# All rows of attention scores in the two double PSUM buffers of a planned decoder layer, and four changed rules of its planner

## The chip, the core and the metric

The kernel runs on one core of a Trainium2 chip. The core has a matrix engine (TensorE; the profile has PE for its matmuls and PEld for its weight loads), a vector engine (VectorE, DVE), a scalar engine (ScalarE, ACT), GpSimd (POOL) and a queue that issues transfers (SyncE, SP). Matmuls write to PSUM, which VectorE and ScalarE read; everything else lies in SBUF. The metric is the time of one execution in microseconds on the device. Each execution is one program, and the profile shows one of them.

## The reference

One decoder layer on 1024 tokens of width 1024: a norm, one input projection, a recurrent branch (convolution, two gates, a scan), a latent attention branch of 8 heads, an output projection over both, a SwiGLU FFN of width 2816, and a gated per-layer embedding. What matters here is the attention:

```python
s = jnp.einsum('bqhd,bkhd->bhqk', qn, k_nope)          # 64 wide
s = s + jnp.einsum('bqhr,bkr->bhqk', qr, k_rope)       # 32 wide
s = jnp.where(k_idx <= q_idx, s * ATT_SCALE, -inf)     # causal
pr = softmax(s, axis=-1)
out = jnp.einsum('bhqk,bkhd->bqhd', pr, v)
```

## The kernel before

Everything is float32. A float32 operand is split into a rounded part and a rest (tiles `x_h` and `x_l`, or `q_h` and `q_l`), and a product is three matmuls: high by high, high by low, low by high. Tiles hold 128 rows of features by 1024 tokens.

The attention works by head (0 to 7) and by block of 128 queries (`qb` 0 to 7). The function `scores` takes one such block: the scores of 128 queries against the `n` = 128 (`qb` + 1) keys that the causal mask leaves, 128 to 1024 columns in PSUM (tile `s`). TensorE writes them in three matmuls of up to 512 columns, or six, with one more of 128 columns that adds the mask (`s<-mb,ib`). VectorE takes the negative maximum of each row (`nm<-s`), and ScalarE the exponential with the row's sum (`pA<-s,nm` for the blocks up to 512 columns, `pB<-s,nm` for the longer ones). Only then may the PSUM buffer of these scores be used again. The exponentials are transposed in blocks of 128 by TensorE (tile `tp`), copied and split by ScalarE and VectorE (tile `pt`), and multiplied with the values into tile `av`, which ScalarE and VectorE then move to `ya`. Beside this run, for the heads to come, the products that make queries (`qps`, then `qf`, `q_h`, `q_l`) and keys (`kps`, then `k_h`, `k_l`), at the start the values (`v`), and at the end the output projection of the recurrent half (`wo`), after its operands were split (`yr_h`, `yr_l`). After each second head its normalisation is spread over the partitions (`rbc`).

PSUM has eight banks of 512 columns. `NWIDE` = 2 (L369) makes four of them two double buffers of 1024 columns (pool `wide`); the other four are single (pool `bank`). Before, a block of scores of over 512 columns takes a double buffer, and one of up to 512 a single bank, from the pool that `tp`, `av`, `qps`, `kps`, `v` and `rbc` use too.

The order of the instructions is not that of the code. The kernel records every operation (`Plan.add`), and `Plan.order` (L239) lays them out by list scheduling, once, before the program is built: it keeps a clock for each engine, takes of the operations that are ready and have their buffers the one with the lowest key (its place in the code, with a few shifts), and lets it last as long as `Plan.cost` says (L167). The table `LAT` (L133) has how much later another engine sees an operation's end: 0.25 us from VectorE to TensorE and 0.11 from ScalarE to TensorE, for instance. A buffer comes free at `b.done`, after its last user (L329). Each engine then runs its own instructions strictly in the order that the plan gave, waiting on semaphores for the others. Since all instructions are emitted in one helper, all have the same line in the profile, L361, and are told apart by their tiles; in the changed kernel, three lines longer there, it is L364.

Of the kernel before, what the change touches and what calls it, by code (L numbers as in the profile page):

```python
# [19 lines left out]
HB = 512  # L20
# [120 lines left out]
class Plan:  # L141
# [25 lines left out]
    def cost(self, eng, fn, a, k, out):  # L167
        w = out.width() if isinstance(out, View) else 0
        if fn == "dma_start":
            v = k["out"] if isinstance(k["out"], View) else k["in_"]  # L170
            return v.shape[0] * v.width() * 4 / 360e3, 2.1
        if eng == "tensor":
            if fn == "transpose":
                return 0.108, 0.18
            return w * 0.000417 + 0.0135, 0.18
        if eng == "vector":
            if fn == "reciprocal":
                return 0.065 + w * 0.0063, 0.13
            if fn in ("tensor_reduce", "reduce_sum"):
                return 0.065 + k["in_"].width() * 0.00104, 0.13  # L180
            ptr = 0.061 * any(isinstance(x, View) for x in (k.get("scalar"), *a[2:])) if fn == "scalar_tensor_tensor" else 0.0
            one = fn in ("tensor_copy", "tensor_scalar", "tensor_scalar_mul", "tensor_scalar_add", "tensor_scalar_max")
            if one and all(v.buf.tag not in PS for v in [*a, *k.values()] if isinstance(v, View)):
                return 0.068 + w * 0.00052, 0.13
            return 0.068 + ptr + w * 0.00104, 0.13
        if eng == "scalar":
            src = k["in_"] if "in_" in k else a[1]
            c = (0.052 if src.buf.tag in PS else 0.093) + w * 0.000833
            c += 0.093 * sum(isinstance(k.get(n), View) for n in ("scale", "bias"))
            c += 0.2 * isinstance(k.get("accum_out"), View)  # L190
            return c, 0.14
        return 0.15 + w * (0.0033 if fn == "tensor_copy" else 0.0022), 0.14
# [10 lines left out]
    def add(self, eng, fn, a, k):  # L203
        o = Op()
        o.eng, o.fn, o.a, o.k, o.idx = eng, fn, a, k, len(self.ops)
        o.succ, o.npred, o.ready = [], 0, 0.0
        out = k["out"] if "out" in k else a[0]
        outs = [v for v in (out, k.get("accum_out")) if isinstance(v, View)]
        rest = list(a[1:] if "out" not in k else a) + [v for n, v in k.items() if n not in ("out", "accum_out")]
        ins = [v for v in rest if isinstance(v, View)]  # L210
        o.cost, o.lat = self.cost(eng, fn, a, k, out)
        o.port = self.shares(eng, fn, ins)
        f = k.get("func") or next((x for x in a if isinstance(x, AF)), None)
        o.table = f.name if eng == "scalar" and f is not None and f.name in FIRST else None
        preds = {self.hold: True} if self.hold else {}
        for v, w in [(v, False) for v in ins] + [(v, True) for v in outs]:
            p0, p1, c0, c1 = v.region
            keep = []
            for (q, r, qw) in v.buf.log:
                hit = r[0] < p1 and p0 < r[1] and r[2] < c1 and c0 < r[3]  # L220
                if hit and (w or qw) and q is not o:
                    preds[q] = True
                if not (w and q is not o and p0 <= r[0] and r[1] <= p1 and c0 <= r[2] and r[3] <= c1):
                    keep.append((q, r, qw))
            keep.append((o, v.region, w))
            v.buf.log = keep
        o.key = o.idx + self.shift + OFF.get(eng[0] + out.buf.name.rstrip('_ab') if isinstance(out, View) else '', 0) + (DEF if eng in ('vector', 'scalar') and not any(v.buf.tag == 'bank' for v in ins + outs) else 0)
        o.bufs = list(dict.fromkeys(v.buf for v in ins + outs))
        for b in o.bufs:
            if not b.left:  # L230
                b.first = o.idx
            b.left += 1
        for q in preds:
            q.succ.append(o)
            o.npred += 1
        self.ops.append(o)
        return o

    def order(self):  # L239
# [28 lines left out]
        while left:  # L268
            while frees and frees[0][0] <= t:
                _, _, tag, n = heapq.heappop(frees)  # L270
                free[tag] += n
            moved = False
            for e in names:
                while future[e] and future[e][0][0] <= t:
                    _, i, o = heapq.heappop(future[e])
                    heapq.heappush(avail[e], (o.key, i, o))
                if busy[e] > t or not avail[e]:
                    continue
                pick, skipped, best = None, [], None
                tries = 0  # L280
                while avail[e] and tries < 40:
                    i, _, o = heapq.heappop(avail[e])
                    tries += 1
                    ok = all(b.placed or free[b.tag] > min(unplaced(b), RES.get(b.tag, 99)) for b in o.bufs)
                    if ok:
                        key = i
                        if e == "scalar" and o.table and o.table not in SAME.get(table, ()):
                            key = i + SWITCH
                        if best is None or key < best[0]:
                            if best is not None:  # L290
                                skipped.append((best[1], best[2].idx, best[2]))
                            best = (key, i, o)
                        else:
                            skipped.append((i, o.idx, o))
                        if e != "scalar" or key == i:
                            break
                    else:
                        skipped.append((i, o.idx, o))
                for s in skipped:
                    heapq.heappush(avail[e], s)  # L300
                if best is None:
                    continue
                o = best[2]
                moved = True
                start = t
                c = o.cost
                if o.port:
                    start = max(t, port)
                    port = start + c
                if o.table and o.table not in SAME.get(table, ()):  # L310
                    table = FIRST[o.table]
                    c += 1.28
                for b in o.bufs:
                    if b.placed:
                        continue
                    b.placed = True
                    free[b.tag] -= 1
                    q, d = queue[b.tag], ahead[b.tag]
                    d[b.pos] = True
                    while head[b.tag] < len(q) and d[head[b.tag]]:  # L320
                        head[b.tag] += 1
                busy[e] = start + c
                o.end = start + c + o.lat
                o.st = start
                out.append((t, o.idx, o))
                left -= 1
                for b in o.bufs:
                    b.left -= 1
                    b.done = max(getattr(b, "done", 0.0), o.end)  # L329
                    if not b.left:  # L330
                        heapq.heappush(frees, (b.done, b.pos, b.tag, 1))
                for s in o.succ:
                    s.npred -= 1
                    r = start + c + (LAT[e, s.eng] if (e, s.eng) in LAT else o.lat)
                    s.ready = max(s.ready, r)
                    if not s.npred:
                        heapq.heappush(future[s.eng], (s.ready, s.idx, s))
            nxt = [busy[e] for e in names if busy[e] > t and (avail[e] or future[e])]
            nxt += [future[e][0][0] for e in names if future[e] and future[e][0][0] > t]
            if frees:  # L340
                nxt.append(frees[0][0])
            nxt = [x for x in nxt if x > t]
            if not left:
                break
            if not nxt:
                raise RuntimeError("the plan does not fit")
            t = min(nxt)
# [22 lines left out]
PS = ("bank", "wide")  # L370
# [6 lines left out]
def hybrid_layer(ctx, tc, xT, pT, pos, vec, const, const2, w1, wn, wrg, wq, wkv, wo, wg, wu, *rest):  # L377
# [252 lines left out]
    for k in range(8):  # L630
# [29 lines left out]
        for i in range(2):  # L660
            c = slice(i * P, (i + 1) * P)
# [215 lines left out]
    def scores(hd, qb):  # L877
# [7 lines left out]
        (qh, ql), (kh, kl) = qs[hd], ks[hd]  # L885
        n = (qb + 1) * P
        cc = slice(qb * P, (qb + 1) * P)
        ps = wide("s") if n > HB else bank("s")
        for c0 in range(0, n, HB):
            c1 = min(c0 + HB, n)  # L890
            T.matmul(ps[:, c0:c1], lhsT=qh[:, cc], rhs=kh[:, c0:c1], start=True, stop=False)
# [608 lines left out]
```

## Time and profile before

| | us |
|---|---|
| median of three timed runs | 1231.26 (1230.91 to 1231.33) |
| the profiled execution | 1228.91 |
| span of its instructions | 1227.1 |
| TensorE busy with matmuls | 1172.6 (96%) |
| VectorE busy | 990.7 (81%) |
| ScalarE busy | 648.5 (53%) |
| GpSimd busy | 249.8 (20%) |

The page's second part cuts the span into 40 slices of 30.7 us:

```profile
PE   8999999999999999999999999999599999999995
DVE  7878777777888699988888888867689758776998
ACT  8347857777855365454454444444232213476665
PEclk9999999999999999999999999999799999999998
```

Each digit is the busy share in tenths, and PEclk the clock that TensorE was granted. The attention is in slices 6 to 11, where VectorE and ScalarE stand at seven to eight tenths as well; the FFN fills slices 13 to 33. A busy share is not a bound by itself: matmuls are pipelined, and the record of one overlaps the next. Waits have to be read from the timeline of a stretch.

### The profile page before, as it was taken

Reading aid. Unit: us, or ns where it says so; the run is one execution under the profiler, and the core shown is the slowest. Engines: PE = TensorE matmul, PEld = TensorE weight load, DVE = VectorE, ACT = ScalarE, POOL = GpSimd, SP = SyncE. Lnnn points to the kernel's source line nnn. Section 1 sums busy time; section 2 is a strip of 40 time slices with the busy share of each in tenths; the row PEclk is TensorE's granted clock in tenths of the full one; section 3 lists DMA queues with packets and bytes.
Section 4 is the critical chain, followed back from the end, with each engine's and each line's share of the span. In section 5 each row is a group of like instructions: output and inputs, shape, how many; then the busy total and the mean of one; then the engine's idle time right before and its main releaser. Section 6 shows DMA issues by size and latency. Waiting matters only on the chain.

```text
span 1227.1 us, 15468 instructions
## 1 busy us (share of the span) xinstructions
PE 1172.6 (96%) x5608; PEld 967.8 (79%) x5608; DVE 990.7 (81%) x1486; ACT 648.5 (53%) x1086; POOL 249.8 (20%) x149
## 2 busy tenths in 40 slices
PE   8999999999999999999999999999599999999995
PEld 6788777878778878888888888888488887887894
DVE  7878777777888699988888888867689758776998
ACT  8347857777855365454454444444232213476665
POOL 0001220322101123333113332133000000243042
PEclk9999999999999999999999999999799999999998
DMA  8001100000214231453434434465998774122362
GB/s 333 18 18 35 35 1 1 1 1 1 87 69 155 103 121 54 170 189 120 172 122 160 182 124 167 155 220 188 382 374 289 276 253 176 35 103 90 117 206 87
DMA packets 50268, 165.35 MB, mean 135 GB/s; under 512 B 5648, under 2 KB 8976, under 8 KB 50192
## 3 DMA queue, kind: packets, MB, share of 16 engines
q1 hardware_dynamic: 50192, 164.37, 36.7%
q8 instruction: 44, 0.72, 0.2%
q14 instruction: 32, 0.26, 0.1%
HBM read 115.58 MB, written 48.76 MB: 134 GB/s over the span
## 4 chain that ended last, share of the span: by engine, by line
PE 76%; DVE 12%; ACT 5%; issue 3%; DMA 3%; POOL 1%; SPq 0%; DVEq 0%; ACTq 0%; POOLq 0%
PE ff_z L361 27%; PE ff_y L361 14%; PE ff_x L361 6%; PE wo L361 4%; PE plg L361 4%; PE wn L361 4%; PE s L361 3%; PE tp L361 2%; PE av L361 2%; DMA wd_r<-in_wd 2%; PE qps L361 2%; PE wn_b L361 1%; DVE h L361 1%; PE wn_a L361 1%; PE wo_a L361 1%
## 5 line engine op out<-in xcount | busy, mean ns | idle before, releaser
L361 POOL TENSOR_TENSOR silu<-silu,nf_rb 128x512 f32<-128x512 f32 x77 | 119.8, 1580 | 280.1 <-DVE silu L361 257.9
L361 PE MATMUL ff_z<-hx,wd 128*128 128x512 f32 x528 | 129.6, 393 | 9.8 <-DVE h L361 8.1
L361 PE MATMUL ff_z<-x,wg 128*128 128x512 f32 x528 | 128.0, 390 | 0.2
L361 PE MATMUL ff_z<-x,wu 128*128 128x512 f32 x528 | 127.0, 389 | 0.9 <-DVE ff_u L361 0.9
L361 PEld LDWEIGHTS ff_z<-hx,wd 128*128 128x128 f32 x528 | 99.7, 189 | 31.9 <-DVE h L361 8.8
L361 PEld LDWEIGHTS ff_z<-x,wu 128*128 128x128 f32 x528 | 99.0, 188 | 21.9 <-DVE ff_u L361 1.3
L361 PEld LDWEIGHTS ff_z<-x,wg 128*128 128x128 f32 x528 | 98.9, 188 | 21.8 <-DVE x L361 1.1
L361 DVE TENSOR_TENSOR h<-ff_z,h 128x512 f32<-128x512 f32 x64 | 44.1, 690 | 33.7 <-PE ff_z L361 25.6
L361 ACT ACTIVATE wd<-wd_r 128x256 fp32r<-128x256 f32 (+2 forms) x64 | 29.8, 490 | 73.6 <-DMA wd_r<-in_wd 26.3
L361 PE MATMUL ff_y<-hx,wd 128*128 128x512 f32 x264 | 66.3, 394 | 0.1
L361 POOL TENSOR_TENSOR p_acc<-p_acc,sq 128x1024 f32<-128x1024 f32 x7 | 18.2, 2596 | 231.8 <-ACT sq L361 231.8
L361 PE MATMUL ff_y<-x,wg 128*128 128x512 f32 x264 | 64.3, 390 | 0.9 <-ACT x L361 0.9
L361 PE MATMUL ff_y<-x,wu 128*128 128x512 f32 x264 | 63.4, 389 | 0.0
L361 PE MATMUL plg<-hg_h,wpg_l 128*128 128x256 f32 (+1 forms) x192 | 61.4, 320 | 1.3 <-DVE wpg_l L361 1.2
L361 PE MATMUL plg<-hg_h,wpg_h 128*128 128x256 f32 (+1 forms) x192 | 61.5, 320 | 0.3 <-ACT np_rb L361 0.3
L361 PE MATMUL plg<-hg_l,wpg_h 128*128 128x256 f32 (+1 forms) x192 | 61.3, 319 | 0.0
L361 PEld LDWEIGHTS ff_y<-hx,wd 128*128 128x128 f32 x264 | 50.2, 191 | 11.4 <-ACT wd L361 0.9
L361 PEld LDWEIGHTS ff_y<-x,wg 128*128 128x128 f32 x264 | 49.4, 188 | 11.7 <-ACT x L361 1.3
L361 ACT ACTIVATE wd<-wd_s 128x256 fp32r<-128x256 f32 (+2 forms) x48 | 23.3, 496 | 66.1 <-DVE wd_s L361 50.6
L361 DVE TENSOR_TENSOR pt<-tp,pt 128x512 fp32r<-128x512 f32 (+1 forms) x96 | 50.3, 549 | 9.6 <-ACT pt L361 9.3
L361 PEld LDWEIGHTS ff_y<-x,wu 128*128 128x128 f32 x264 | 49.6, 188 | 10.3
L361 DVE TENSOR_REDUCE nm<-s 128x1 f32<-128x128 f32 (+3 forms) x64 | 47.8, 752 | 11.7 <-PE s L361 10.8
(407 smaller groups left out, 3041.0 us busy)
## 6 DMA issues: line engine op xcount, KB each, us to landing
hx<-hx SPq DMA_DIRECT2D x154, 512.0 KB, 3.9
wpg_raw<-in_wpg SPq DMA_DIRECT2D x24, 512.0 KB, 3.5
wg_r<-in_wg SPq DMA_DIRECT2D x22, 512.0 KB, 4.6
wu_r<-in_wu SPq DMA_DIRECT2D x22, 512.0 KB, 4.1
wn_raw<-in_wn SPq DMA_DIRECT2D x10, 512.0 KB, 7.2
wo_raw<-in_wo SPq DMA_DIRECT2D x8, 512.0 KB, 4.0
h<-in_xT SPq DMA_DIRECT2D x8, 512.0 KB, 4.2
hd<-h SPq DMA_DIRECT2D x8, 512.0 KB, 2.9
```

The costliest lines, as they stand in the source:

```text
L361: getattr(self.engines[o.eng], o.fn)(*a, **k)
```

## The change

Four edits, three of them in the planner:

- a matmul is reckoned at 0.113 us at least, where one of 128 columns was at 0.067;
- an operation of VectorE or ScalarE of which an input starts at another partition than its output is reckoned 0.11 us longer (`k_h`, `k_l` and `ya`, which move between the halves of the partitions);
- a PSUM buffer whose last user is not TensorE comes free when `LAT` says that TensorE sees it, where before it was when the operation's own latency was over: for VectorE 0.25 us behind its end and not 0.13, for ScalarE 0.11 and not 0.14;
- every block of scores takes one of the two double buffers, whatever its size.

```diff
@@ cost
         if eng == "tensor":
             if fn == "transpose":
                 return 0.108, 0.18
-            return w * 0.000417 + 0.0135, 0.18
+            return max(w * 0.000417 + 0.0135, 0.113), 0.18
@@ add
         o.cost, o.lat = self.cost(eng, fn, a, k, out)
+
+        if eng in ("vector", "scalar") and any(v.region[0] != outs[0].region[0] for v in ins if v.width() > 8):
+            o.cost += 0.11
         o.port = self.shares(eng, fn, ins)
@@ order
-                    b.done = max(getattr(b, "done", 0.0), o.end)
+                    b.done = max(getattr(b, "done", 0.0), start + c + LAT[e, "tensor"] if b.tag in PS and e != "tensor" else o.end)
@@ scores
-        ps = wide("s") if n > HB else bank("s")
+        ps = wide("s")
```

The instructions are the same ones. What moves is their order on TensorE, VectorE and ScalarE from the last input projection to the end of the attention, and a few of them in the last tenth of the program; the orders of GpSimd and SyncE are the same in both. Three places show it.

TensorE at the start of the attention, before: the scores of head 0's blocks of 128 and 256 queries by keys (`s`), among the projections of the values (`v`). Rows of three matmuls are one projection; three of them stand ahead of these rows.

```order
497 L361 MATMUL v<-wkv_h,ckv_l 128x512
498 L361 MATMUL s<-k_h,q_h 128x128
499 L361 MATMUL s<-k_l,q_h 128x128
500 L361 LDWEIGHTS ib
501 L361 MATMUL s<-mb,ib 128x128
502 L361 MATMUL s<-k_h,q_l 128x128
503 L361 MATMUL v<-wkv_h,ckv_h 128x512
504 L361 MATMUL v<-wkv_l,ckv_h 128x512
505 L361 MATMUL v<-wkv_h,ckv_l 128x512
506 L361 MATMUL s<-k_h,q_h 128x256
```

The same place in the changed kernel; four projections stand ahead of these rows.

```order
500 L364 MATMUL v<-wkv_h,ckv_h 128x512
501 L364 MATMUL v<-wkv_l,ckv_h 128x512
502 L364 MATMUL v<-wkv_h,ckv_l 128x512
503 L364 MATMUL s<-k_h,q_h 128x128
504 L364 MATMUL s<-k_l,q_h 128x128
505 L364 LDWEIGHTS ib
506 L364 MATMUL s<-mb,ib 128x128
507 L364 MATMUL s<-k_h,q_l 128x128
508 L364 MATMUL s<-k_h,q_h 128x256
509 L364 MATMUL s<-k_l,q_h 128x256
```

The first two blocks of scores have moved behind the fifth projection and stand next to each other.

TensorE in the middle of the attention, before: the first blocks of head 5's scores, of 128, 256, 384 and 512 columns.

```order
981 L361 MATMUL s<-k_h,q_l 128x128
982 L361 MATMUL s<-k_h,q_h 128x256
983 L361 MATMUL s<-k_l,q_h 128x256
984 L361 LDWEIGHTS ib
985 L361 MATMUL s<-mb,ib 128x128
986 L361 MATMUL s<-k_h,q_l 128x256
987 L361 MATMUL s<-k_h,q_h 128x384
988 L361 MATMUL s<-k_l,q_h 128x384
989 L361 LDWEIGHTS ib
990 L361 MATMUL s<-mb,ib 128x128
991 L361 MATMUL s<-k_h,q_l 128x384
992 L361 MATMUL s<-k_h,q_h 128x512
```

The same blocks in the changed kernel.

```order
1008 L364 MATMUL s<-k_h,q_l 128x128
1009 L364 MATMUL s<-k_h,q_h 128x256
1010 L364 MATMUL s<-k_l,q_h 128x256
1011 L364 LDWEIGHTS ib
1012 L364 MATMUL s<-mb,ib 128x128
1013 L364 MATMUL s<-k_h,q_l 128x256
1014 L364 MATMUL tp<-cs,pB 128x128 x4
1015 L364 MATMUL rbc<-cs,rx_2435 128x128 x3
1016 L364 MATMUL s<-k_h,q_h 128x384
1017 L364 MATMUL s<-k_l,q_h 128x384
1018 L364 LDWEIGHTS ib
1019 L364 MATMUL s<-mb,ib 128x128
```

The four blocks stood in one burst; now four transposes of exponentials and three of the normalisation (`rbc`) stand between the 256 and the 384 columns, and more behind the 384.

ScalarE at the same place, before: the exponentials of these blocks (`pA`), the copies of transposed ones (`pt`), of queries (`q_h`) and of outputs (`ya`).

```order
215 L361 ACTIVATE pA,rs<-s,nm 128x128
216 L361 ACTIVATE pt<-tp 128x384
217 L361 ACTIVATE pA,rs<-s,nm 128x256
218 L361 ACTIVATE pt<-tp 128x256
219 L361 ACTIVATE pA,rs<-s,nm 128x384
220 L361 ACTIVATE pt<-tp 128x128
221 L361 ACTIVATE q_h<-qf 128x512
222 L361 ACTIVATE pt<-tp 128x512
223 L361 ACTIVATE ya<-av 64x512
224 L361 ACTIVATE pA_2569,rs<-s,nm 128x512
```

And in the changed kernel.

```order
223 L364 ACTIVATE pA,rs<-s,nm 128x128
224 L364 ACTIVATE pt<-tp 128x512
225 L364 ACTIVATE q_h<-qf 128x512
226 L364 ACTIVATE pA,rs<-s,nm 128x256
227 L364 ACTIVATE pA,rs<-s,nm 128x384
228 L364 ACTIVATE ya<-av 64x512
229 L364 ACTIVATE sq<-ya 128x1024
230 L364 ACTIVATE pA_2588,rs<-s,nm 128x512
```

Between the exponentials of 128 and 256 columns there are now a copy of 512 columns and one of the queries, where a copy of 384 stood; those of 256 and 384 are neighbours, where a copy stood between them.

## Rows read from the trace of the kernel before

**Rows 1.** Stages: stretch (us), its length, each engine's busy us (instructions), clock, DMA.

```profile
165.13:351.35 186.22, 177.81 (x1035) 144.19 (x1034) 148.57 (x254) 139.56 (x293) 38.39 (x24) 0.98 0.08 26
351.35:368.86 17.51, 14.39 (x75) 11.45 (x74) 11.69 (x19) 8.61 (x10) 0.00 (x0) 1.00 0.00 1
...
322.80:351.35 28.55, 27.73 (x166) 22.53 (x165) 28.39 (x39) 22.77 (x40) 4.30 (x2) 1.00 0.41 145
```

**Rows 2.** Stretches with idle TensorE, and two at half clock: same columns.

```profile
168.00:176.00 8.00, 5.91 (x21) 3.82 (x19) 4.81 (x13) 6.09 (x13) 2.37 (x1) 0.79 0.01 2
171.50:174.90 3.40, 3.40 (x10) 2.54 (x10) 0.45 (x2) 1.97 (x5) 2.37 (x1) 0.50 0.02 5
204.00:212.00 8.00, 6.28 (x31) 4.59 (x30) 5.94 (x12) 4.68 (x11) 1.27 (x1) 0.81 0.00 0
209.00:212.40 3.40, 3.40 (x13) 2.48 (x13) 2.36 (x5) 1.37 (x6) 0.00 (x0) 0.50 0.00 0
228.00:236.00 8.00, 6.98 (x40) 5.03 (x38) 5.60 (x15) 7.77 (x17) 0.00 (x0) 1.00 0.00 0
248.00:256.00 8.00, 7.25 (x45) 5.73 (x44) 6.96 (x13) 5.67 (x14) 1.77 (x2) 1.00 0.00 0
272.00:276.00 4.00, 3.59 (x27) 3.01 (x25) 2.91 (x7) 3.58 (x9) 0.00 (x0) 1.00 0.00 0
288.00:300.00 12.00, 11.13 (x61) 8.17 (x60) 9.90 (x18) 9.41 (x22) 1.73 (x2) 1.00 0.00 0
316.00:320.00 4.00, 3.35 (x21) 2.30 (x21) 2.85 (x8) 3.46 (x11) 0.00 (x0) 1.00 0.10 16
332.00:336.00 4.00, 3.18 (x19) 2.12 (x18) 4.00 (x8) 3.56 (x7) 0.00 (x0) 1.00 0.14 39
```

**Rows 3.** Timeline of head 5's first scores: start, us, engine, instruction, idle before.

```profile
274.28 0.29 DVE L361 TENSOR_REDUCE nm<-s 128x1 f32<-128x128 f32 x1 [0.65 <-PE s L361]
...
274.41 0.36 PE L361 MATMUL s<-k_h,q_l 128*128 128x256 f32 x1
...
274.67 0.37 ACT L361 ACTIVATE pA<-s,nm 128x128 f32<-128x128 f32 x1
...
275.18 0.44 PE L361 MATMUL s<-k_h,q_h 128*128 128x384 f32 x1 [0.41 <-ACT pA L361]
```

**Rows 4.** TensorE's waits, 165.13 to 351.35: us in total, times, longest.

```profile
PE s L361 <- DVE v L361: 1.8, 1, 1.8
PE s L361 <- ACT pA L361: 1.4, 3, 0.6
...
PE s L361 <- DVE ya L361: 0.8, 1, 0.8
PE s L361 <- DVE pt L361: 0.8, 2, 0.4
```

**Rows 5.** Timeline at the start of the attention.

```profile
165.33 1.22 DVE L361 TENSOR_TENSOR zg<-wn,nx_rb 128x1024 f32<-128x1024 f32 x1 [2.77 <-PE wn L361]
...
167.94 1.21 DVE L361 TENSOR_TENSOR rg_h<-rg_h,zg 128x1024 f32<-128x1024 f32 x1
...
169.07 1.74 DVE L361 TENSOR_TENSOR v<-v 128x256 fp32r<-128x256 f32 x5
...
170.29 0.36 PE L361 MATMUL s<-k_h,q_h 128*128 128x256 f32 x1 [1.77 <-DVE v L361]
```

**Rows 6.** Pieces of the chain that ended last: start, us, what.

```profile
165.29 2.04 PE v L361 x9
...
260.02 0.87 PE tp L361 x8
```

**Rows 7.** Timeline of head 2's first scores.

```profile
203.06 1.39 DVE L361 TENSOR_TENSOR k_l<-kps,k_h 64x512 fp32r<-64x512 f32 x2 [0.66 <-ACT k_h L361]
...
208.93 1.16 DVE L361 TENSOR_TENSOR pt<-tp,pt 128x512 fp32r<-128x512 f32 x2
...
208.95 0.56 PE L361 MATMUL s<-k_h,q_h 128*128 128x256 f32 x1 [0.83 <-DVE ya L361]
```

## The prediction

> **What bounds the kernel now.** I read the table of stages first, then the stretches in which TensorE stands still, then who releases it there. The change alters the order of work only from the last projections to the end of attention (and in a handful of places at the very end), so the stage that counts is 165.13 to 351.35, from the first value projection to the last head's broadcast: 186.22 us, in which TensorE is busy for 177.81, VectorE for 148.57 and ScalarE for 139.56 [rows 1]. TensorE is the bound, with two engines close behind that it hands work to and gets buffers back from. In the last part of it, 322.80 to 351.35, VectorE is busy for 28.39 of 28.55 us as well [rows 1]. Behind the stage nothing is to be had: in the next 17.51 us TensorE works 14.39 us on output projections that are the same in both kernels [rows 1], and in the slices of the page the FFN behind that stands at nine tenths or more throughout. What the stage saves arrives at the end of the kernel one for one.
>
> So the prize is what TensorE loses inside the stage. Its visible idle time is 186.22 - 177.81 = 8.4 us, and it stands in a few places [rows 2]: 2.1 us at 168 to 176, 1.7 at 204 to 212, 1.0 at 228 to 236, and 0.4 to 0.9 at five more. After the first two the granted clock is 0.50 for 3.4 us each (1.2 instead of 2.4 GHz), with TensorE fed throughout [rows 2]: that costs up to 1.7 us each time. A wait also costs more than its idle time shows, since a matmul's record is longer than the spacing of two: the wait before the 384-column score shows 0.41 us, but its start comes 0.77 us after that of a 256-column matmul that needs 0.11 at 2.4 GHz [rows 3], so 0.66 are lost, 0.25 of them unseen. In all some 8.4 + 3.4 and 3 to 4 us unseen: about 15 us is the most that any order can give.
>
> Who ends these waits: TensorE's scores wait 4.8 us, on VectorE for v, ya and pt and on ScalarE for pA [rows 4]. All of these hand back a single bank to a short score. No row has a score waiting for ScalarE's pB, which is what hands back a double buffer.
>
> **The change, part by part.** No instruction is added or removed; only order and buffers change, so each engine's work is the same and only waits count. The queues of SyncE and GpSimd keep their order whole. The edits act together on one planned order, so I price places, not edits.
>
> *The start (168 to 176).* Before, the 256-column score waits 1.77 us for a bank that VectorE frees only after rg_h (1.21 us) and two value rows [rows 5]. Now five value projections stand ahead of it, and it takes the double buffer that zg gives back at 166.55 (165.33 + 1.22) [rows 5]. Worked forward: nine matmuls of the projections take 2.04 us [rows 6], three belong to each, so five of them from 165.13 end at 168.5, and the two scores (four matmuls each, some 0.45 us) near 169.45. The sixth projection wants the second one's bank: VectorE ends zg at 166.55, the first value row 0.7 later (five pieces, two a row, take 1.74), rg_h, for which zg must first pass ScalarE, near 168.9, the second row at 169.6 [rows 5], so with the release it waits until about 169.9, 0.4 us. The next user finds VectorE behind by as much again, and waits about 0.6. Idle is 1.0 instead of 2.1, the unseen part some 0.3 less, and two short waits rather than one long one should leave the clock up: 1.1 + 0.3 + 1.7 = 3.1 us gained.
>
> *Head 2 (204 to 212).* The score waits 0.83 us for the bank of av, which ya frees [rows 7]; with a double buffer it does not, and with the unseen part that is 1.0. The wait of 0.9 before it, for VectorE's k_l and pt, is a matter of order: VectorE's k_l take 1.39 us for two where pt take 1.16 [rows 7], the 0.11 us each that the plan now counts; I leave that wait in. The fall of the clock behind them goes or stays: half of 1.7. Gained: 1.85.
>
> *The later heads.* Idle time between 228 and 336 in the six stretches is 1.02 + 0.75 + 0.41 + 0.87 + 0.65 + 0.82 = 4.5 us [rows 2]. About 2.7 of it (1.0, 0.3, 0.4, 0.35 and 0.65) stands in bursts of short scores like that of rows 3; the rest is waits for VectorE that I leave in. With 0.25 us unseen on some five waits, 3.8 us are to be had. What takes their place is the wait for the double buffer: the 384 score now takes the one of the 128 score, free after nm (0.29) and pA (0.37, and an accumulator read behind it) [rows 3], the same release as before. The difference is that the plan has put seven transposes between, 0.76 us by the 0.87 of eight [rows 6].
>
> *The new wait, bound from both sides.* 64 scores in two buffers make 62 reuses in place of 30. From below: the 30 reuses of before cost nothing, as no score waits for pB [rows 4]; below zero a reuse can't cost. From above: the 32 short scores paid 4.8 us for their banks, 0.15 each [rows 4], which would be 9.3 us. I take 0.05, 3.1 us, nearer to the row of the same kind of buffer. ScalarE's queue is what stands in the way of more: in head 5, the exponential of 256 columns now has a copy of 512 and q_h ahead of it, where a copy of 384 stood.
>
> *The rest.* The few instructions moved at the end of the kernel (four transposes by one matmul, one multiplication by e) I cost at nothing: they lie beside a busy TensorE, and the matmul that they pass is under 0.2 us.
>
> Sum: 3.1 + 1.85 + 3.8 - 3.1 = 5.65 us. The profiled execution took 1228.91 us (span 1227.1), so 1223.3 by it; the median of the three timed runs is 2.35 us above that execution, and 1231.26 - 5.6 gives **1225.7 us**.
>
> **The rivals.** *More goes.* The double buffers never stall, as now: 5.65 + 3.1 = 8.75 us, and some of the waits that I left in go too, since the plan now counts the late release behind VectorE: 9 to 12 us, 1219 to 1222. For it: the wide rows of before, none of which waits. Against: with 62 reuses the room between two is a third of what it was.
>
> *Nothing is left.* The waits only move, from banks to double buffers at 0.14 us a reuse (8.75 / 62), or to VectorE, whose full last 28.55 us [rows 1] absorb what the heads before save. Time 1231, give or take 2. For it: VectorE is at 80% over the stage. Against: it is idle for 186.22 - 148.57 = 37.65 us of the stage, all but 0.16 of them ahead of 322.80 [rows 1], room to be earlier in.
>
> *Slower.* Two buffers for all scores make one ring: TensorE writes, VectorE takes the maximum, ScalarE the exponential, and only then may the next but one begin. In ScalarE's queue the exponentials stand behind copies that themselves wait for TensorE's transposes. If each reuse costs 0.20 us, which is above the 0.15 that the banks cost, that is 12.4 - 8.75 = 3.7 us more than now. And TensorE then pauses shortly all the time: it is after pauses that the clock fell at 171.5 and 209 [rows 2]. Each further fall costs 1.7, so with one or two falls it is 1235 to 1239; take 1237. It decides from 0.14 us a reuse. Against it: 1.02 us of pauses between 228 and 236 left the clock at 1.00 [rows 2].
>
> The Trainium skill, in "TensorE: Matmul & The Clock Gate", section "A second HAM failure mode: psum-queue depth-cycling", says that a kernel which cycles through PSUM buffers lets TensorE idle briefly between groups of matmuls so often that its clock swings between the two levels. By that rule the last rival would be the likely one; this case's trace agrees with it at two places of some ten and not at the others.
>
> *The plan does not do what it says.* The numbers in the edit could be off: the copies from one half of the partitions to the other do take 0.11 us more in VectorE [rows 7], so that part is real. A release put too late would only make the plan looser; it would land in the second case.
>
> **How the numbers follow.** Forecast, a gain of 2.5 to 9 us: 0.57. More: 0.11. Nothing: 0.15. Slower: 0.17. A difference of under 0.2%, 2.5 us, can't be told from none here. Faster by more than that is 0.57 + 0.11 = 0.68, within it 0.15, slower 0.17. The likeliest case alone runs from 1222 to 1229; the range for 8 in 10 takes the near halves of the others, 1219.5 to 1234.
>
> **What would show it.** Right: the first two stretches lose their idle time and the fall of the clock at 171.5; no score waits for v or ya; the stage from the first value projection to the last broadcast is 178 to 183 us; the stages behind it are unchanged in length. Wrong: rows in which scores wait for pA and pB by the dozen, 0.15 us or more each; more than two stretches at half the clock; or the same stage length with VectorE as the one waited for.

## The result and the profile after

The changed kernel takes **1216.42 us** (median of four runs, 1212.98 to 1217.57) against 1231.09 for the kernel before beside it (1229.4 to 1231.33): a ratio of 0.9879, with a 95% interval of 0.9857 to 0.9901. That is 14.7 us faster, where I forecast 5.65 and gave a lower end of 1219.5. The direction was right, the size was not.

The stage of attention, from the first value projection to the end of the last product with the values, answers to [rows 1]. The columns are the same: stretch, length, busy time of PE, PEld, DVE, ACT and POOL with instructions, clock, DMA.

```profile
150.40:167.77 17.37, 15.33 (x61) 12.51 (x61) 13.10 (x17) 8.99 (x14) 5.99 (x3) 0.90 0.00 0
167.77:339.32 171.55, 169.79 (x1032) 141.59 (x1031) 147.13 (x254) 138.02 (x293) 36.09 (x23) 1.00 0.09 29
339.32:357.57 18.25, 15.07 (x78) 11.96 (x77) 11.51 (x18) 8.63 (x10) 0.00 (x0) 1.00 0.00 0
```

The stage is 186.22 - 171.55 = 14.67 us shorter. TensorE's idle time in it went from 186.22 - 177.81 = 8.41 to 171.55 - 169.79 = 1.76 us, and the clock is at 1.00 throughout. The first line is the stretch ahead of it, in which only some projections changed places: it lies at 0.90, since in this one execution the clock fell there (below). The third is the stretch behind it, 0.7 us longer than before (17.51), with 78 matmuls in place of 75. Three matmuls of the output projection (`wo`) that stood inside the stage now stand behind it. So 0.7 of the 14.67 us is work that moved, and stage and stretch together are 203.73 - 189.80 = 13.93 us shorter.

The profiled executions are 13.1 us apart (1228.91 and 1215.79), less than the stage alone: this one began 1.1 us late (its last key rotation, `kr`, ends at 150.40, before at 149.30), lost 1.5 in that fall and 0.7 behind the stage, and won back 1.8 in the FFN and later, 1.2 of it around a wait of 0.9 us for VectorE's `ff_u` (842.72 to 862.80 before) that is not there now. That the medians lie 14.67 us apart, just as the stages do, is chance.

The stretches of the starts of heads 0, 2, 3, 4, 5, 6 and 7, and of the last head's end, answer to [rows 2]; same columns.

```profile
169.00:177.00 8.00, 7.53 (x38) 5.92 (x37) 6.48 (x17) 7.80 (x15) 2.41 (x1) 1.00 0.01 2
203.60:211.60 8.00, 8.00 (x57) 7.08 (x55) 6.29 (x13) 6.64 (x18) 0.91 (x1) 1.00 0.00 0
222.00:234.00 12.00, 11.43 (x78) 9.69 (x77) 8.94 (x22) 11.16 (x24) 1.36 (x2) 1.00 0.00 1
243.50:251.50 8.00, 7.93 (x51) 6.39 (x49) 6.95 (x15) 5.90 (x14) 1.29 (x1) 1.00 0.00 1
265.00:272.00 7.00, 7.00 (x50) 6.15 (x49) 5.85 (x13) 5.78 (x15) 1.02 (x1) 1.00 0.00 0
284.00:296.00 12.00, 11.78 (x77) 9.67 (x76) 10.40 (x21) 9.61 (x23) 2.57 (x2) 1.00 0.00 0
305.00:313.00 8.00, 8.00 (x57) 7.03 (x56) 6.66 (x14) 6.59 (x15) 1.29 (x1) 1.00 0.41 133
320.00:326.00 6.00, 5.96 (x36) 4.80 (x35) 6.00 (x9) 5.82 (x12) 0.00 (x0) 1.00 0.11 27
```

Only the first and the third keep an idle half microsecond. All of TensorE's waits in the stage, of 0.2 us and more, which answer to [rows 4] (us in total, times, longest):

```profile
PE v L364 <- DVE v L364: 0.5, 1, 0.5
PE nr_bc L364 <- DVE ya L364: 0.5, 1, 0.5
PE tp L364 <- DVE ya L364: 0.3, 1, 0.3
PE qps L364 <- DVE pt L364: 0.2, 1, 0.2
```

No score is among them. The timeline of head 5's first scores answers to [rows 3] (start, us, engine, instruction, idle before it).

```profile
268.95 0.37 PE L364 MATMUL s<-k_h,q_l 128*128 128x256 f32 x1
...
269.14 0.37 ACT L364 ACTIVATE pA<-s,nm 128x128 f32<-128x128 f32 x1 [0.41 <-DVE nm L364]
269.15 0.60 PE L364 MATMUL tp<-cs,pB 128*128 128x128 f32 x4
...
269.41 0.19 ACT L364 ACTIVATION_READ_ACCUMULATOR pA<-s,nm 128x1 f32 x1
...
269.59 0.49 PE L364 MATMUL rbc<-cs,rx 128*128 128x128 f32 x3
...
269.83 0.42 PE L364 MATMUL s<-k_h,q_h 128*128 128x384 f32 x1
```

The 384-column score takes the double buffer of the 128-column one, which the accumulator read gives back at 269.41 + 0.19 = 269.60. TensorE is busy with the seven transposes of the plan until the score starts at 269.83: the wait of 0.41 us [rows 3] is filled. It is not so everywhere. This is the tightest kind of reuse, in head 3, on the queue of weight loads:

```profile
229.63 0.37 ACT L364 ACTIVATE pA<-s,nm 128x128 f32<-128x128 f32 x1
...
229.90 0.19 ACT L364 ACTIVATION_READ_ACCUMULATOR pA<-s,nm 128x1 f32 x1
...
230.14 0.19 PEld L364 LDWEIGHTS s<-k_h,q_h 128*128 128x128 f32 x1 [0.35 <-ACT pA L364]
230.14 0.44 PE L364 MATMUL s<-k_h,q_h 128*128 128x384 f32 x1
```

The buffer is free at 229.90 + 0.19 = 230.09 and the next score starts 0.05 us later: here it waits. TensorE's product ahead of it (`nr_bc`, 0.52 us from 229.51) ends at 230.03, so TensorE itself loses 0.11 us, too little for the list of waits. I took the same distance, from the last reader's end to the first matmul of the next but one block, for all 62 reuses: five are at 0.05 to 0.06 us, eighteen under 0.25, half are over 0.8. So many reuses are tight, as I feared, but the weight loads of scores wait for `pA` only twice, 0.5 us together:

```profile
PEld s L364 <- ACT pA L364: 0.5, 2, 0.4
```

The 30 reuses of before have one such wait on the same queue:

```profile
PEld s L361 <- ACT pB L361: 0.3, 1, 0.3
```

### The profile page after: what moved, and what is told of

Same layout as the page of the kernel before. It is cut to its first block, busy times and chain, and to the rows that moved or that the text cites. A ratio compares the mean times of both kernels' runs of the same rounds, so it can differ in the third digit from the quotient of the medians.

```text
span 1214.0 us, 15474 instructions
## 1 busy us (share of the span) xinstructions
PE 1166.5 (96%) x5608; PEld 967.5 (80%) x5608; DVE 985.3 (81%) x1486; ACT 647.3 (53%) x1086; POOL 250.3 (21%) x149
## 4 chain that ended last, share of the span: by engine, by line
PE 83%; DVE 9%; ACT 3%; DMA 2%; issue 2%; POOL 1%; SPq 0%; DVEq 0%; ACTq 0%; POOLq 0%
PE ff_z L364 27%; PE ff_y L364 14%; PE ff_x L364 7%; PE plg L364 6%; PE wo L364 4%; PE s L364 4%; PE wn L364 4%; PE av L364 2%; PE tp L364 2%; PE g L364 2%; PE wn_b L364 2%; PE qps L364 2%; DMA wd_r<-in_wd 1%; PE wn_a L364 1%; DVE h L364 1%
## 5 line engine op out<-in xcount | busy, mean ns | idle before, releaser
L364 DVE TENSOR_TENSOR hx<-silu,hx 128x512 fp32r<-128x512 f32 x55 | 56.4, 1033 | 0.6 <-ACT hx L364 0.6
L364 ACT ACTIVATE silu<-silu 128x512 f32<-128x512 f32 x44 | 27.7, 634 | 52.7 <-POOL silu L364 47.9
```

What stands on the lines that cost most here:

```text
L364: getattr(self.engines[o.eng], o.fn)(*a, **k)
```

## The experiments

The stage is the stretch between the same two instructions in each run's profile; where the clock does not fall inside it, its length hardly depends on the execution (171.55 and 171.52 us in two profiles of the changed kernel). Falls inside it are in the numbers: two of 3.4 us each in before and before nudged, one in each of the two runs with half of the short blocks in banks, none in the others. The stage of before and of the three single banks holds two to four `wo` matmuls more than the others', 0.5 to 0.9 us.

| run | median us | ratio to before, 95% | stage us |
|---|---|---|---|
| before | 1231.0 to 1231.9 | | 186.22 |
| changed | 1216.42 | 0.988 (0.986 to 0.990) | 171.55 |
| buffers alone | 1218.18 | 0.990 (0.988 to 0.991) | 172.98 |
| planner's rules alone | 1230.42 | 0.999 (0.998 to 1.001) | 182.69 |
| before, nudged | 1229.71 | 0.998 (0.997 to 1.000) | 184.5 |
| changed, nudged | 1218.18 | 0.989 (0.987 to 0.990) | 172.37 |
| changed, again | 1217.44 | 0.989 (0.987 to 0.991) | 171.52 |
| three single banks | 1251.58 | 1.016 (1.014 to 1.019) | 188.19 |
| 128 and 256 in banks | 1222.04 | 0.993 (0.991 to 0.995) | 177.13 |
| 384 and 512 in banks | 1225.06 | 0.995 (0.993 to 0.997) | 178.24 |
| buffers held longer | 1223.30 | 0.993 (0.992 to 0.995) | 177.09 |
| same load, not held | 1224.69 | 0.995 (0.993 to 0.996) | 178.57 |
| two alive, in banks | 1229.50 | 0.998 (0.997 to 1.000) | 183.09 |

**The buffers alone.**

```diff
-        ps = wide("s") if n > HB else bank("s")
+        ps = wide("s")
```

> Only the buffers: every block of scores in a double buffer, the planner's three rules as before. The full change gave 14.7 us (1231.1 to 1216.4), its stage from the first value projection to the last broadcast 171.6 us where it was 186.2. Theory 'buffers' (the short scores no longer wait for single banks that copies and projections hold): 11 to 15 us faster than before, stage 172 to 175. Theory 'planner' (the truer costs keep TensorE fed, the buffers alone make waits for pA and pB): 0 to 4 us faster, scores waiting for pA or pB at ten places or more. Theory 'order by chance' (any other order of this list would have lost less than the one before): anything between, 4 to 10.

It took 1218.18 us, 13.4 less than before. The stage and the largest of its waits:

```profile
165.25:338.23 172.98, 170.46 (x1032) 141.72 (x1031) 147.18 (x254) 138.01 (x293) 37.57 (x24) 1.00 0.09 28
...
PE tp L364 <- DVE k_l L364: 0.7, 2, 0.4
```

The one line brings 186.22 - 172.98 = 13.24 of the stage's 14.67 us. No score has a wait in its list. What the planner's rules add is the rest: the waits of transposes behind VectorE's `k_l`, 0.7 us here, are among those that are gone in the full change.

**The planner's rules alone.**

```diff
+            return max(w * 0.000417 + 0.0135, 0.113), 0.18
+            o.cost += 0.11
+            ... start + c + LAT[e, "tensor"] if b.tag in PS and e != "tensor" else o.end
         ps = wide("s") if n > HB else bank("s")
```

> Only the planner's three rules (matmul floor, 0.11 us between partitions, release of a PSUM buffer behind its reader); short scores in single banks as before. Theory 'buffers': 0 to 4 us faster than before, scores still waiting for v, ya, pt or pA for 3 us or more in all. Theory 'planner': 8 to 13 us faster. Theory 'order by chance': 4 to 10 us faster.

It took 1230.42 us, which can't be told from before.

```profile
165.44:348.13 182.69, 172.03 (x1032) 142.18 (x1031) 148.69 (x254) 138.51 (x293) 37.60 (x24) 1.00 0.08 27
...
PE s L364 <- ACT pA L364: 4.0, 5, 1.0
PE s L364 <- ACT q_h L364: 1.6, 1, 1.6
PE s L364 <- DVE v L364: 1.5, 1, 1.5
PE qps L364 <- ACT pA L364: 1.4, 1, 1.4
```

The clock did not fall in this stage at all, and still only 3.5 us are gained, 0.7 of them moved `wo`: two falls (3.4 us) are missing, while 182.69 - 172.03 = 10.66 us of idle time are left, more than the 8.41 of before. Whether the new order kept the clock up or this one execution did, one profile can't tell. The short scores wait for their banks again, 1.0 us at a time. The line `qps <- pA` is the other side: a product of queries waits for a bank that a short score holds.

**Is it any other order?** Both kernels with one number of the plan moved.

```diff
-                return 0.108, 0.18
+                return 0.110, 0.18
```

> The kernel before, with one number of the plan nudged: a transpose reckoned 0.110 us long in place of 0.108. That makes nothing truer, but moves the order from the attention on as the change does. Theories 'buffers' and 'planner': within 2 us of before. Theory 'order by chance': 5 us or more from before, most likely faster, as the order before would be an unlucky one.

> The changed kernel with the same nudge: a transpose reckoned 0.110 us long in place of 0.108. Theories 'buffers' and 'planner': within 2 us of the changed kernel, 1214 to 1219. Theory 'order by chance': 5 us or more slower than it.

They took 1229.71 and 1218.18 us, each within 2 us of its own kernel. Put beside each other by tile names, the traces of before and before nudged have some 360 of 5608 matmuls in another place, as many as the full change moves. In the changed kernel the nudge moved some 40. So an order by chance is worth 1 to 2 us in the two that were tried, not 14.

The changed kernel's nudge shows that a reuse can still cost something. In head 3 one score waits for a double buffer:

```profile
PE s L364 <- ACT pA L364: 1.4, 1, 1.4
```

There ScalarE loads its table for exponentials (`ACT_TABLE_LOAD`, 1.28 us from 228.76) ahead of the exponential that the score waits for. In the changed kernel the same load starts at 228.34, and TensorE has other work nearly all the while: it is the place at 230.14 above.

> The changed kernel once more, beside the others of this set: all theories 1214 to 1219. It says how much of the 1.8 us between it and the buffers alone (1218.2) is the planner's: 'the planner's rules are worth nothing on top' 1217 to 1219, 'they are worth some 2 us' 1215 to 1217. The clock fell at 153.1 in its first profile, after a wait of 2.2 us that stands in both kernels; if that is a matter of the run, this profile may show no fall there.

It took 1217.44 us (1215.42 to 1219.74), inside the first of the two expectations and near its edge, so it does not decide between them: what the planner's rules add to the buffers is 0.7 to 1.8 us by the medians and 1.4 by the stage, no more than the nudge moves. The profile has no fall of the clock at 153, so that belongs to the execution.

**Own wait or room for the others?** One single bank less.

```diff
-        return plan.tile(psp, [P, HB], F32, name, "bank", 8 - 2 * NWIDE)
+        return plan.tile(psp, [P, HB], F32, name, "bank", 7 - 2 * NWIDE)
```

> The changed kernel with three single banks in place of four (one bank of PSUM is left unused). Theory 'own wait' (the gain is that a short score no longer waits for a bank of v, av or tp): the scores still wait for nothing, and the other tiles run as before on three banks: within 3 us of the changed kernel. Theory 'room for the others' (the gain is that tp, av, qps and v have the four banks for themselves, and run ahead): the loss of one gives back most of it, 8 us or more, with waits of tp, av and qps for ScalarE's and VectorE's pt, and none of scores.

It took 1251.58 us. The whole program uses these banks: the stage begins 9.3 us later than before and 9.9 us more are lost behind it. Inside the stage 188.19 - 171.55 = 16.6 us are lost (0.7 of them `wo`), more than the change had won:

```profile
PE qps L364 <- DVE k_l L364: 1.6, 1, 1.6
PE s L364 <- POOL q_l L364: 1.5, 1, 1.5
PE s L364 <- ACT pB L364: 1.5, 3, 0.9
PE tp L364 <- DVE pt L364: 1.2, 3, 0.8
PE av L364 <- ACT pt L364: 0.9, 2, 0.5
```

The waits of `qps`, `tp` and `av` come as the room theory has it; scores wait too, against it. I read that as what they need (`q_l`, and exponentials behind late copies) being late, which no run tests. That the other tiles need all four banks is shown; that a short score in one of them acts as such a bank less is the reading that fits.

**Half of the short blocks.**

```diff
-        ps = wide("s")
+        ps = wide("s") if n > 256 else bank("s")          # the one run
+        ps = bank("s") if 256 < n <= HB else wide("s")    # the other
```

> The changed kernel, but the blocks of 128 and 256 columns take single banks as before; those of 384 and up the double buffers (16 of the 32 short blocks moved). In the trace before, waits stood ahead of scores of 256, 384 and 512 columns; 384 the most often. Theory 'each block pays for its own wait': a half to two thirds of the gain, 1221 to 1225. Theory 'a burst of more than two short blocks is what fills the banks': two short blocks in banks are harmless, 1215 to 1219.

> The changed kernel, but the blocks of 384 and 512 columns take single banks as before; those of 128 and 256 take the double buffers. It is the other half of the run with 128 and 256 in banks, whose stage was 177.1 us: 5.6 longer than the changed kernel's. Theory 'each block in a bank pays for itself': the halves add up to the stage of the planner's rules alone (182.7, 11.2 longer), so this one is 4 to 7 us longer, 175.5 to 178.5, and the time 1221 to 1225. Theory 'the first two blocks in double buffers are enough' (the starts of the bursts wait the least then): within 2 us of the changed kernel, stage under 173.5. Theory 'the longer blocks are the costly ones': as slow as with all in banks, stage 180 to 184.

They took 1222.04 and 1225.06 us (the second 0.06 above what was expected); the stages are 5.6 and 6.7 us longer than the changed kernel's, 12.3 together, where all short blocks in banks (the planner's rules alone) cost 11.1. So the cost goes about with the number of blocks in banks. In both, one fall of the clock (1.7 us each) is in these numbers; without the two falls the halves make 8.9. In the second run scores wait only 0.5 us in all. Its largest wait is another tile's, and the clock fell behind it:

```profile
PE tp L364 <- DVE pt L364: 2.4, 1, 2.4
```

That is a loss of the kind that the room theory asks for, nearly without waits of the scores themselves.

**Does the reuse cost?** Another reader keeps each buffer longer.

```diff
         A.activation(pd[:, :n], ps[:, :n], AF.Exp, bias=nm[:, qb:qb + 1], accum_out=rs[:, qb:qb + 1])
+        V.tensor_add(small([P, 1], "jk"), ps[:, :1], rs[:, qb:qb + 1])                # held longer
+        V.tensor_add(small([P, 1], "jk"), nm[:, qb:qb + 1], rs[:, qb:qb + 1])         # same load, not held
```

> The changed kernel with one more reader of each block of scores: VectorE adds the row's sum to one column of it, behind the exponential (64 additions of 128x1, into a tile that nobody reads). The buffer comes free some 0.3 to 0.8 us later at each of 62 reuses. Theory 'the reuse is tight' (0.05 us each as it stands, as I forecast): the later release is paid for at most of them, 10 us or more slower than the changed kernel, scores waiting for VectorE's new addition. Theory 'the plan leaves room' (between two scores of one buffer lies 2.5 us of other work of TensorE): under 3 us slower.

> The changed kernel with the same 64 additions on VectorE as in the run that held the buffers longer, but of the block's negative maximum in place of a column of the scores: the same work for VectorE, and no later release. That run was 5.9 us slower than the changed kernel (1223.3 against 1217.4; stage 177.1 us against 171.5), with one wait of 1.5 us for the addition and 6.4 us more busy time on VectorE. Theory 'later release' (the buffers' hold is what cost): within 2 us of the changed kernel, stage 171 to 173.5. Theory 'VectorE's load' (its 6 us delay pt, k_l and ya): 1221 to 1224, stage 175 to 178.

The first took 1223.30, between the two expectations. The buffer comes free 0.19 us later at the least and 0.44 in the median, counted from the exponential's end to the addition's. From the addition's end to the next but one score's start the shortest distance is again 0.05 us, and 20 of 62 are under 0.25: the scores follow the later release as tightly as they followed the exponential. The second, in which nothing is held longer, took 1224.69, with a stage of 178.57; time and stage lie 0.6 to 0.7 us above the upper ends of the theory of VectorE's load. Their stages, first and second:

```profile
164.92:342.01 177.09, 171.93 (x1031) 140.57 (x1030) 153.53 (x318) 137.83 (x293) 37.63 (x24) 1.00 0.08 28
...
PE s L364 <- DVE jk L364: 1.5, 1, 1.5
```

```profile
166.98:345.55 178.57, 172.53 (x1033) 141.01 (x1032) 159.94 (x318) 137.45 (x293) 36.03 (x23) 1.00 0.09 27
...
PE tp L364 <- DVE pt L364: 2.0, 4, 0.9
PE tp L364 <- DVE k_l L364: 1.4, 3, 0.7
```

The load on VectorE is enough for a loss of this size: 12.8 us more of it (159.94 - 147.13) lengthen the stage by 7.0, with waits for `pt` and `k_l`, not for scores' buffers. The control is not clean, since its additions take longer than those of the first run (12.8 us more of VectorE's time against 6.4; in both, 1.8 of it are slower `yr_l` splits, see the last section). By 0.55 us lost per us of load, the first run's 6.4 make 3.5 of its 5.5; some 2 us are left for the later release, an estimate, of which a wait of 1.5 us for `jk` is seen. That is 0.03 us a reuse. By this estimate VectorE, more than the two buffers, is what stands next to TensorE now.

**Broken bursts or room?** Short scores in banks, but a block is placed only while fewer than two others are alive. The lines that count `alive` are left out here.

```diff
-  ok = all(b.placed or free[b.tag] > min(unplaced(b), RES.get(b.tag, 99)) for b in o.bufs)
+  ok = all(b.placed or free[b.tag] > min(unplaced(b), RES.get(b.tag, 99)) and (b.name != "s" or alive < 2) for b in o.bufs)
```

> The planner's three rules, the short scores in single banks as before, and a limit in the plan: a block of scores of any size is placed only when fewer than two others are not yet free. So at most two blocks are alive, as with the double buffers, but a short one still takes a bank from tp, av and qps. Theory 'spread' (the gain is that the bursts of short scores are broken up): most of the gain, 1216 to 1221, stage 172 to 176. Theory 'room' (the gain is that no short score takes one of the four banks): like the planner's rules alone, 1227 to 1232, stage 180 to 185.

It took 1229.50 us, with the stage and its largest wait:

```profile
165.96:349.05 183.09, 173.30 (x1033) 142.42 (x1032) 149.09 (x254) 138.76 (x293) 37.63 (x24) 1.00 0.08 27
...
PE s L367 <- ACT pA L367: 4.6, 5, 1.3
```

That is the planner's rules alone again (182.69). In the trace more than two blocks are alive for 1.7 us only, and never more than three; with the planner's rules alone it was up to six. So the bursts are no cause of their own: with two scores alive the time is 1229.5 if the short ones sit in banks, and 1216.4 if they sit in the double buffers.

## Why the prediction was wrong

*What held.* TensorE's waits in the stage were the prize, and the stretch behind it is longer only by the three matmuls that moved there. The bound of about 15 us "that any order can give" stands: 13.93 of it were taken, and 1.76 us of idle time are left. The waits of scores for banks that `v`, `ya`, `pt` and `pA` hand back are gone. There is no fall of the clock in the stage, no score waits for `v` or `ya`, and the seven transposes fill the wait in head 5.

*The terms.* Taken by kind over all places, my sum stands so beside the traces:

| term | forecast | measured |
|---|---|---|
| idle time removed | 1.1 + 0.83 + 2.7 = 4.6 | 8.41 - 1.76 = 6.65 |
| falls of the clock | 1.7 + 0.85 = 2.55 | 2 x 1.7 = 3.4 |
| unseen part of waits | 1.6 | 14.67 - 6.65 - 3.4 - 0.7 = 3.9 |
| `wo` matmuls that moved behind the stage | 0 | 0.7 |
| new waits for double buffers | -3.1 | about 0: no score in PE's list; 0.5 on the weight loads, before 0.3 |
| sum | 5.65 | 14.67 |

Of the 9.0 us that the sum lacks, 3.1 are the new wait, 2.0 idle time (0.5 of it at the start, where 0.47 us are left of the 1.0 that I worked out) and 2.3 the unseen part of waits that I left in, 0.85 half a fall of the clock, and 0.7 the moved matmuls. Two steps failed.

**The first step that failed** is "The new wait": 62 reuses at 0.05 us. I priced a reuse between what waits for banks had cost and zero, by a guess nearer to zero. The only rows of the same kind were the 30 reuses of before, and they said zero on PE; the measured value is that row. The plan reckons with a buffer's release (it has the exponential and its latency in its costs), and puts other ready work of TensorE there, as the timeline of head 5 shows for one. Eighteen distances under 0.25 us cost next to nothing: a short distance is not a wait. That holds for this order; in the nudged one a single reuse cost 1.4 us. The prediction also said that 62 reuses in place of 30 leave a third of the room between two; it is about half.

**The second, and the larger**, is in "Head 2" and "The later heads": the waits for VectorE that I left in. Some 1.5 us of their idle time went, and 2.3 us more of the unseen part than I counted. I took a wait's releaser for its cause. These are the waits of before that I meant:

```profile
PE tp L361 <- DVE k_l L361: 0.8, 2, 0.5
...
PE tp L361 <- DVE pt L361: 0.7, 1, 0.7
PE av L361 <- DVE pt L361: 0.7, 1, 0.7
```

VectorE is named where `tp` and `av` wait for `pt`, but a transpose that came late for want of a bank makes `pt` late in turn. That this chain is the cause is argued. That the waits for `pt` go with the banks is shown: of 1.4 us the buffers alone leave 0.2 us each of `av` and `qps`. Those for `k_l` stay there, at 0.7 us, and are gone in the changed kernel's order. The run with the planner's rules alone has `qps` waiting 1.4 us for `pA`, and the one with three banks makes such waits by hand. My reading is that with four banks to themselves `tp`, `av`, `qps` and `v` run ahead, and VectorE and ScalarE get their work earlier. In head 7, where I saw VectorE full for the last 28.55 us, 35.43 us from the first score to the end became 30.78, with 191 matmul records in place of 203. Three of the twelve are the `wo` that moved behind the stage; the rest of that work is now done earlier.

*The unseen part* I bounded at 3 to 4 us, and it was 3.9, but I counted it only for the waits that I took out: 1.6. It was some six tenths of the idle time that went with it. (In the later heads 2.7 us and five times 0.25 make 3.95, where the prediction has 3.8.)

*The clock* I gave one and a half falls back, and none is left in the stage: 0.85 us. None of the six profiles with all short blocks in double buffers and four banks has a fall in the stage, but of the four with all of them in banks two have none either, so how much of this is the order's is open.

*The rivals.* "More goes", at 0.11, was the true one in its condition (the double buffers hardly stall) and too small in its price, 9 to 12 us, since it too let some of the waits for VectorE stand. "Slower" needed 0.14 us a reuse and fell. The Trainium skill, in "TensorE: Matmul & The Clock Gate", section "A second HAM failure mode: psum-queue depth-cycling", tells of a kernel in which cycling through PSUM leaves TensorE idle for short times so often that its clock swings. This trace does not show that: 64 blocks go through two buffers, five reuses with 0.05 to 0.06 us between reader and writer, but TensorE is idle for 1.76 us in all and its clock is at 1.00 over all 171.55 us. The Trainium skill's "Perfetto Trace Analysis", section "Optimization Strategy", says that the same gap coming back again and again on the busiest engine can mean that buffers are short. That agrees with rows 2 and 4, in which gaps stand at the starts of seven of the eight heads, and I did not draw its conclusion for the tiles that weren't scores.

*Open.* What a later release costs by itself: the control loaded VectorE more than the run that it was for. And how much of the planner's 1.4 us is any one rule's: a nudge of one number moves as much.

## What to carry to other kernels

When short-lived tiles share a pool with the pipeline that feeds the bottleneck, count what the pool's other users lose, not only the short tile's own wait: here one line that moved 32 of them to two buffers with room was worth 13 us, while truer planner costs without it were worth nothing that could be measured. A releaser that appears in many waits at the same places can be a sign of short buffers upstream, so try one buffer less as well as one more, since it shows at once who needs them. And charge a planned reuse what the same kind of reuse costs in the trace, even if that is zero, with a wider range for what another order may do to it.

## What was not expected of the hardware

The granted clock fell after the same wait in some executions and not in others. In all twelve profiles with four banks TensorE waits 2.0 us for the products of keys near 150 us, and in three of them (one is the changed kernel's first) the clock falls to 0.50 for 3.4 us within 2 us behind it; around the end of the wait at the start of the output projection (2.5 us, with three banks 3.1) it fell in five of thirteen.

```profile
153.10:156.50 3.40, 3.40 (x10) 2.62 (x9) 3.37 (x4) 3.34 (x7) 1.00 (x1) 0.50 0.00 0
```

This one made the stretch ahead of the stage 1.5 us longer (17.37 against 15.83), one at the output projection the stretch behind it 0.5 (18.73 against 18.25, two executions of the changed kernel). So small differences between single executions say nothing without the clock beside them.

In the kernel before, one of the four splits `yr_l` on VectorE took 3.00 us, while the others took 1.28:

```profile
328.94 2.38 POOL L361 TENSOR_TENSOR y_acc<-y_acc,sq 128x1024 f32<-128x1024 f32 x1 [3.14 <-ACT sq L361]
...
329.40 3.00 DVE L361 SCALAR_TENSOR_TENSOR yr_l<-rg_h,vc,yr_h 128x1024 fp32r<-128x1024 f32 x1
```

GpSimd's addition runs until 328.94 + 2.38 = 331.32, and the split ends 1.08 us behind that, a little less than its own length: it seems to have stood still for most of the addition. The Trainium skill, "GPSIMD Engine Reference", section "1. Specifications", says that GpSimd shares its way into SBUF with VectorE, and that they get in each other's way when VectorE's instruction has two inputs there; this row agrees. In the changed kernel all four take 1.27 to 1.28 us, a part of VectorE's relief in head 7 that I had not forecast. In the two runs with additions on VectorE the four take 6.9 us again, as before (6.8), in place of 5.1.
